# First hidden chunk by plain products, first keys beside the gates, and additions of the down product given priority

## The chip, the cores and the metric

The kernel runs on one core of one Trainium2 chip. The metric is device time in microseconds (us), the median of several executions of the whole program on that core. Three executions of the kernel before gave 1960.85, 1961.96 and 1962.16 us. Engines are named as in the profile: PE (TensorE), PEld (its weight load), DVE (VectorE), ACT (ScalarE), POOL (GpSimd), SP (SyncE, which issues the transfers). A label such as L132 is line 132 of the kernel.

## What is computed

A two-layer encoder over 768 tokens (512 of a prompt, 256 of a sample) of width 1024. Layer 0 mixes tokens by a Fourier transform, layer 1 by a gated delta rule with 8 heads. Behind each mixer stands a SwiGLU block with 2816 hidden units, and each block has a modulated RMS norm ahead of it. All in float32. Cut to what the change touches:

```
def swiglu(h, w_gu, w_down):
    gu = h @ w_gu
    return (silu(gu[..., :2816]) * gu[..., 2816:]) @ w_down

mod = (silu(c) @ ada_w[layer] + ada_b[layer])
sh1, sc1, g1, sh2, sc2, g2 = split(mod, 6)
h = rmsnorm(x, norm_mix_g[layer]) * (1 + sc1) + sh1
x = x + g1 * mixer(h)
h = rmsnorm(x, norm_ffn_g[layer]) * (1 + sc2) + sh2
x = x + g2 * swiglu(h, w_gu[layer], w_down[layer])
```

In the gated delta rule `proj = h @ w_in` gives queries, keys, values, an output gate and 32 columns of gates for the recurrence (4 x 8).

## The kernel before

**Products.** A float32 product is made of three passes in the type fp32r: each operand is split into a high part (a rounded copy, made by ACT) and a low part (the difference, made by DVE or POOL), and PE adds high by high, low by high and high by low in one bank of PSUM (`passes`). Weights come from HBM into a staging tile `stg`, are cast to `wh` by ACT (L151) and to `wl` by DVE (L152), and live in one of five slots (WP = 5) until PE has used them. Matmuls go through the helper at L132. In the changed kernel the same lines are L130, L149 and L150.

**The block of hidden units.** The hidden units are worked through in 22 chunks of 128, in groups that PARTS lists: in layer 0 mostly four chunks at a time, in layer 1 first two, then fours. For each chunk `gate_up` makes gate and up together as a two by two product over halves of the width and halves of the tokens (384 columns each), in a Strassen-Winograd form: 7 half products, each 12 matmuls of 384 columns, 84 in all where the plain form needs 96. Its operand blocks numbered 1 to 7 are made once for a layer by `norm_blocks`: the normalised rows m = 0 to 7 (one of them is 128 features by 768 tokens), the differences of row halves, and the high and low part of each. Blocks 1 and 2 are rows as they are; the others are differences of rows. In each layer the first group is the chunks 0 and 1 side by side, so that PE has two products for every operand that arrives.

**`norm_blocks`.** It takes squares of x, sums them over the features with a product by ones, and then for each m multiplies by the root (L349, on DVE, for m = 7 on POOL), applies scale and shift in two ACT instructions (L352), casts the high part (L199, ACT) and takes the low part (L200, DVE or POOL: the tuples YP, BL and GL name which go to POOL). The order of m is 0, 4, 1, 5, 2, 6, 3, 7, and differences are interleaved.

**The down product.** For each group of four chunks `down4` multiplies by the down weights, in two halves of 512 output columns each; a half is again 7 half products of 12 matmuls, whose results are added into x by `into` (L532, on DVE) as soon as each is complete. A later half product goes on in the same bank of PSUM, so it waits for that addition. Each half runs after the gate and up product of a later chunk, between two of them. Weight casts for down are L497 and L498; differences of weights for gate and up are L379 (one of them on DVE, two on POOL).

**Order.** The order of instructions on each engine is made by a scheduler from the order of the code and priorities: a piece in `tc.high_priority()` goes ahead of others that are ready. Weight casts (L151, L152, L497, L498) and weight differences (L379) have it; the additions at L532 have not. Layer 0 also does the products of the modulation for later blocks (`ada_steps`, tiles `at` of 128 x 512, two matmuls of 256 columns each), which `advance(steps, n)` in `between` deals out among the chunks and the scheduler places.

**Start of the gated delta rule.** The gates product (`pab`, weights at column 4128 - 128) is written first; the queries, keys and values of head h come from `conv_block(h, which, ...)`, one product each.

Of the kernel before, what the change touches and what calls it, by code (L numbers as in the profile page):

```python
# [12 lines left out]
F32 = mybir.dt.float32  # L13
F32R = mybir.dt.float32r
AF = mybir.ActivationFunctionType
# [28 lines left out]
PAIRS = (1, 3, 5)  # L44
YP = (7,)
BL = (0, 1, 2, 3)
GL = (3,)
ST = 4
M7 = 2
WP = 5  # L50
# [59 lines left out]
def encoder_kernel(  # L110
# [87 lines left out]
    def split_to(ah, al, src, eng=None):  # L198
        A_.copy(ah, src)  # L199
        (eng or V).tensor_tensor(al, src, ah.bitcast(F32), ALU.subtract)  # L200
# [133 lines left out]

    def norm_blocks(n, xs, psp, wk, ext, load=True, pairs=False):
# [8 lines left out]
        ts = []  # L344
        for c in range(HK):
            ts.append([])
            for b in range(2):
                t, m = scratch(), c + b * HK
                (G if m in YP else V).tensor_tensor(t, xs[m], rs, ALU.mult)  # L349
                ts[c].append(t)  # L350
                for g, (a, ln) in enumerate(SEGS):
                    A_.activation(t[:, a : a + ln], t[:, a : a + ln], AF.Identity, bias=modT[:, SH[n], m, g : g + 1],  # L352
                                  scale=amod[:, n, m, g : g + 1])
                if b == 0:
                    u, v = 12 + c // 2, slice((c % 2) * HT, (c % 2 + 1) * HT)
                    split_to(eh[u][:, v], el[u][:, v], t[:, lo], G if c in BL else V)
                else:
                    split_to(eh[c], el[c], t, G if c in GL else V)
        for c in range(HK):
            ta, tb = ts[c]  # L360
            t12, t34 = scratch(), scratch()
            V.tensor_tensor(t12[:, lo], ta[:, hi], ta[:, lo], ALU.subtract)
            G.tensor_tensor(t34[:, lo], tb[:, hi], ta[:, hi], ALU.subtract)
            V.tensor_tensor(t12[:, hi], tb[:, hi], t12[:, lo], ALU.subtract)
            G.tensor_tensor(t34[:, hi], tb[:, lo], t12[:, hi], ALU.subtract)
            split_to(eh[4 + c], el[4 + c], t12)
            split_to(eh[8 + c], el[8 + c], t34)
# [5 lines left out]
        return {1: b11, 2: half(0, lo), 3: half(0, hi), 5: half(4, lo), 6: half(4, hi), 7: half(8, lo), 4: half(8, hi)}  # L373

    def gate_up(wgu, ms, blocks, psp, wk):
# [50 lines left out]
        lefts = [left(m) for m in ms]  # L426
        sg = [wk.tile([P, T], F32, name="sg", bufs=3) for _ in ms]
        up = [wk.tile([P, T], F32, name="up", bufs=2) for _ in ms]
# [20 lines left out]
        step(((3, px, False, gate2),))  # L449
        return sg, silu[-1]  # L450

    def residual(x, ps, gate, m):
# [24 lines left out]
    def down4(l, c0, m0, rights, xs, psp, wk):  # L477
# [51 lines left out]
        def into(m, ps, a, b, g):  # L529
            x = xs[m][:, a:b]  # L530
            o = HT if a >= HT else 0
            V.scalar_tensor_tensor(x, ps[:, a - o : b - o], modT[:, gate, m, g : g + 1], x, ALU.mult, ALU.add)  # L532

# [25 lines left out]

    def ffn(l, blocks, xs, psp, wk, gt, between, last, done):  # L560

# [18 lines left out]
        for c0, cn in PARTS[l]:  # L580
# [43 lines left out]
    with ExitStack() as l0:  # L624
# [114 lines left out]
        with ExitStack() as fs:  # L739
# [5 lines left out]
            ppr = fs.enter_context(tc.tile_pool(name="ppr0b", reuse_waits="tile", bufs=6, space=PSUM))  # L745
            blocks = norm_blocks(1, xs, ppr, gt, ext)
            steps = ada((5, 7, 6, 8, 10, 9, 11, 13, 12), psm, apool, 2)
            ffn(0, blocks, xs, ppr, wk, gt, lambda n: advance(steps, n), None,
                lambda m: nc.sync.dma_start(xd[m], xs[m]))
# [9 lines left out]
    with ExitStack() as gs:  # L759
# [141 lines left out]
        def conv_block(h, which, pool, tag, bufs):  # L901
            wb = load_block(win, 0, KC, which * D + h * P)
            pq = product(ppr, wb, hh, hl, KC, tick)
            wc = [cwT[:, d * 24 + which * 8 + h : d * 24 + which * 8 + h + 1] for d in range(5)]
# [288 lines left out]
    with ExitStack() as l1:  # L1193
# [15 lines left out]
        blocks = norm_blocks(3, xs, ppr, gt, ext, False, True)  # L1209

# [77 lines left out]

        ffn(1, blocks, xs, ppr, wk, gt, lambda n: None, finish, None)

# [24 lines left out]
```

## Time and profile before

| what | value |
|---|---|
| median of three executions | 1961.96 us |
| the profiled execution's own time | 1961.55 us |
| span of the profiled execution | 1959.8 us |
| busy ACT, POOL | 977.8 us (50%), 563.7 us (29%) |
| granted PE clock, mean | 0.984 |
| PE products by the high part of a hidden chunk (`pr<-g,wh`, down) | 1072 matmuls, 23.6 us idle before them |

The time stands 1.75 us over the span of the same execution. Busy shares overlap: engines work at the same time, and what sets the time is the engine that the others wait for. In the profile "idle before <- releaser" is how long an engine sat still before an instruction and which instruction let it go on. PEclk is the clock that PE was granted, 1.00 being the full one.

### The profile page before, as it was taken

What the parts mean: (1) busy time and instruction counts of PE and PEld (TensorE: products, weight loads), DVE (VectorE), ACT (ScalarE), POOL (GpSimd) and SP (SyncE); (2) the same over time, 40 slices, a digit from 0 to 9 for tenths busy, and PEclk for the clock granted to TensorE, in tenths of its full rate; (3) what the DMA queues carried; (4) which work ended last, traced back from release to release, by engine and by line L of the source; (5) the groups of instructions that cost most, each with busy time, mean ns of one, the idle gap of its engine ahead of it and who ended that gap; (6) DMA issues with size and microseconds to landing.
All of it is one profiled execution on the core that took longest, in us unless ns stands there. A gap on an engine that the chain in (4) does not pass through costs nothing.

```text
span 1959.8 us, 30027 instructions
## 1 busy us (share of the span) xinstructions
PE 1842.1 (94%) x11281; PEld 1636.7 (84%) x11281; DVE 1468.8 (75%) x2399; ACT 977.8 (50%) x1858; POOL 563.7 (29%) x454
## 2 busy tenths in 40 slices
PE   8899999999999998999999999899789999999998
PEld 5585998888897986888888888778589999999998
DVE  4638877777786767896887787773778888888875
ACT  3526544444443535756656557543554444444543
POOL 1314333233242310122213212320432333433431
PEclk9999999999999998999999999999899999999999
DMA  7654334433425434421222222241213222222211
GB/s 268 215 183 140 86 97 130 127 116 114 139 87 153 126 113 141 119 51 56 69 60 65 66 62 57 61 142 38 53 41 89 68 77 72 65 65 68 77 50 65
DMA packets 231914, 189.72 MB, mean 97 GB/s; under 512 B 20304, under 2 KB 200665, under 8 KB 231769
## 3 DMA queue, kind: packets, MB, share of 16 engines
q1 hardware_dynamic: 231360, 187.66, 31.7%
q8 instruction: 88, 1.44, 0.3%
q14 instruction: 57, 0.47, 0.1%
q10 hardware_dynamic: 409, 0.15, 0.0%
HBM read 174.36 MB, written 13.42 MB: 96 GB/s over the span
## 4 chain that ended last, share of the span: by engine, by line
PE 69%; DVE 14%; ACT 6%; DMA 5%; issue 3%; POOL 3%; ACTq 0%; SPq 0%; DVEq 0%; POOLq 0%
PE pr L132 58%; PE sm L132 8%; DVE wl L152 3%; DVE wa L913 2%; DMA at<-in_ada_w_dram 1%; PE ax L132 1%; DMA cc<-solved 1%; ACT wh L151 1%; POOL yy L1158 1%; DVE we L858 1%; PE big L132 1%; DVE x L532 1%; DVE tmp L1030 1%; ACT we L859 1%; DMA at<-in_final_ada_w_dram 1%
## 5 line engine op out<-in xcount | busy, mean ns | idle before, releaser
L132 PE MATMUL pr<-hh,wh 128*128 128x384 f32 (+2 forms) x1520 | 525.4, 348 | 9.0 <-ACT sg L403 2.3
L132 PE MATMUL pr<-hl,wh 128*128 128x384 f32 (+2 forms) x1520 | 522.8, 344 | 5.2 <-DVE hl L200 4.2
L132 PE MATMUL pr<-hh,wl 128*128 128x384 f32 (+2 forms) x1520 | 520.7, 343 | 1.2 <-DVE wl L152 1.2
L151 ACT CAST wh<-stg 128x512 fp32r<-128x512 f32 (+1 forms) x380 | 230.7, 609 | 394.7 <-PE pr L132 324.3
L152 DVE TENSOR_TENSOR wl<-stg,wh 128x512 fp32r<-128x512 f32 (+1 forms) x380 | 315.2, 832 | 127.7 <-ACT wh L151 124.7
L132 PEld LDWEIGHTS pr<-hh,wh 128*128 128x128 f32 x1520 | 287.7, 190 | 39.8 <-issue 7.4
L132 PEld LDWEIGHTS pr<-hl,wh 128*128 128x128 f32 x1520 | 288.2, 190 | 32.3 <-issue 9.5
L132 PEld LDWEIGHTS pr<-hh,wl 128*128 128x128 f32 x1520 | 287.9, 190 | 24.0 <-issue 6.2
L132 PE MATMUL pr<-g,wh 128*128 128x384 f32 (+2 forms) x1072 | 278.3, 341 | 23.6 <-DVE x L532 13.3
L132 PEld LDWEIGHTS pr<-g,wh 128*128 128x128 f32 x1072 | 191.8, 188 | 37.0 <-DVE x L532 19.8
L379 POOL TENSOR_TENSOR s<-stg 128x512 f32<-128x512 f32 x44 | 62.6, 1423 | 453.4 <-DMA stg<-in_ffn_w_gu_dram 362.7
L132 PE MATMUL pr<-el,wh 128*128 128x384 f32 x528 | 179.9, 341 | 6.4 <-POOL el L200 5.9
L132 PE MATMUL pr<-eh,wh 128*128 128x384 f32 x528 | 181.1, 344 | 3.7 <-ACT eh L199 3.7
L132 PE MATMUL pr<-g,wl 128*128 128x384 f32 (+2 forms) x536 | 181.1, 338 | 0.0
L132 PE MATMUL pr<-eh,wl 128*128 128x384 f32 x528 | 179.2, 339 | 0.0
L498 DVE TENSOR_TENSOR wl<-stg,wh 128x512 fp32r<-128x512 f32 x108 | 99.8, 924 | 36.0 <-ACT wh L497 33.8
L913 DVE SCALAR_TENSOR_TENSOR wa<-pad,cwT,wa 128x770 f32<-128x770 f32 x96 | 109.4, 1140 | 5.2 <-ACT wa L910 3.6
L132 PEld LDWEIGHTS pr<-eh,wh 128*128 128x128 f32 x528 | 100.2, 190 | 12.4 <-issue 7.0
L132 PEld LDWEIGHTS pr<-el,wh 128*128 128x128 f32 x528 | 99.9, 189 | 9.7 <-POOL el L200 8.5
L497 ACT CAST wh<-stg 128x512 fp32r<-128x512 f32 x108 | 67.1, 621 | 81.5 <-PE pr L132 67.1
L132 PEld LDWEIGHTS pr<-g,wl 128*128 128x128 f32 x536 | 101.0, 188 | 0.7
L132 PEld LDWEIGHTS pr<-eh,wl 128*128 128x128 f32 x528 | 99.8, 189 | 0.9 <-issue 0.8
(370 smaller groups left out, 3241.8 us busy)
## 6 DMA issues: line engine op xcount, KB each, us to landing
stg<-in_ffn_w_gu_dram SPq DMA_DIRECT2D x88, 512.0 KB, 4.7
at<-in_ada_w_dram SPq DMA_DIRECT2D x112, 256.0 KB, 3.1
at<-in_ada_w_dram SPq DMA_DIRECT2D x40, 512.0 KB, 4.6
stg<-in_ffn_w_down_dram SPq DMA_DIRECT2D x36, 512.0 KB, 3.7
stg<-in_gdn_w_in_dram SPq DMA_DIRECT2D x33, 512.0 KB, 4.3
at<-in_final_ada_w_dram SPq DMA_DIRECT2D x32, 256.0 KB, 3.6
raw<-gcd SPq DMA_DIRECT2D x8, 768.0 KB, 4.4
stg<-in_fnet_w_dram SPq DMA_DIRECT2D x8, 512.0 KB, 5.1
```

Source lines behind the costliest of these rows:

```text
L132: return nc.tensor.matmul(out, lhsT, rhs, start=start, stop=stop, **kw)
L151: A_.copy(wh[:, :n], src)
L152: V.tensor_tensor(wl[:, :n], src, wh[:, :n].bitcast(F32), ALU.subtract)
L379: eng.tensor_tensor(out, a, b, op)
L497: A_.copy(wh, src)
L498: V.tensor_tensor(wl, src, wh.bitcast(F32), ALU.subtract)
L532: V.scalar_tensor_tensor(x, ps[:, a - o : b - o], modT[:, gate, m, g : g + 1], x, ALU.mult, ALU.add)
L858: V.tensor_scalar(e, src, -44.0, None, ALU.max)
L859: A_.activation(e, e, AF.Exp, scale=-1.0)
L913: V.scalar_tensor_tensor(acc, pad[:, d : d + T + 2], wc[d], acc, ALU.mult, ALU.add)
L1030: se.tensor_tensor(t, r4[:, :, : k + 1, k : k + 1].to_broadcast(sh), u4[:, :, k : k + 1, k + 1 :].to_broadcast(sh), ALU.mult)
L1158: G.tensor_tensor(so, so, sq, ALU.add)
```

## The change

Four edits.

1. The first chunk of each layer is made by a new function, `gate_up_whole`: the plain product, 96 matmuls. Its four results (gate and up, two halves of the tokens) are written k by k, so that the 12 matmuls of a row m can run when that row's high and low parts are there. `norm_blocks` calls it through `early`, between the plain rows and the differences, and takes m in the order 0 to 7. The next group is then chunks 1 and 2 side by side in layer 0, and chunk 1 alone in layer 1.
2. In `norm_blocks` POOL loses the multiplication for m = 7 and five low parts in each layer; they go to DVE. The two differences per row on POOL stay.
3. `into` gets `tc.high_priority()`.
4. The gates product and the first keys' product (both segments of the gates, the first segment of the keys) are written pass by pass beside each other; `conv_block(0, 1)` makes only the second segment.

```diff
-            V.scalar_tensor_tensor(x, ps[:, a - o : b - o], modT[:, gate, m, g : g + 1], x, ALU.mult, ALU.add)
+            with tc.high_priority():
+                V.scalar_tensor_tensor(x, ps[:, a - o : b - o], modT[:, gate, m, g : g + 1], x, ALU.mult, ALU.add)
...
+    def gate_up_whole(wgu, m, plain, psp, wk):
+
+        ws = [load_block(wgu, 0, KC, o + m * P) for o in (0, FFN)]
+        ps = [[bank(psp)[:, :HT] for _ in range(2)] for _ in ws]
+        gens = [passes(p, w, [a[i][0] for a in plain], [a[i][1] for a in plain], skip_group_check=True)
+                for w, pair in zip(ws, ps) for i, p in enumerate(pair)]
+        for _ in zip(*gens):
+            pass
+        sg = wk.tile([P, T], F32, name="sg", bufs=SGB)
+        for i, (a, b) in enumerate(zip(*ps)):
+            v = sg[:, i * HT : (i + 1) * HT]
+            A_.activation(v, a, AF.Silu)
+            V.tensor_tensor(v, v, b, ALU.mult)
+        return sg
...
-            for ms in [(0, 1), *((m,) for m in range(2, cn))] if c0 == 0 else [(c0 + i,) for i in range(cn)]:
+            groups = [(c0 + i,) for i in range(cn)]
+            if c0 == 0:
+                take(0, first)
+                between(AD[0])
+                groups = [(1, 2), *groups[3:]] if cn > 2 else groups[1:]
+            for ms in groups:
...
+        ts, plain = [], []
+        for m in range(KC):
+            t, c = scratch(), m % HK
+            V.tensor_tensor(t, xs[m], rs, ALU.mult)
+            ts.append(t)
+            for g, (a, ln) in enumerate(SEGS):
+                A_.activation(t[:, a : a + ln], t[:, a : a + ln], AF.Identity, bias=modT[:, SH[n], m, g : g + 1],
+                              scale=amod[:, n, m, g : g + 1])
+            if m < HK:
+                u, v = 12 + c // 2, slice((c % 2) * HT, (c % 2 + 1) * HT)
+                split_to(eh[u][:, v], el[u][:, v], t[:, lo])
+                split_to(eh[8 + c][:, hi], el[8 + c][:, hi], t[:, hi])
+                plain.append(((eh[u][:, v], el[u][:, v]), (eh[8 + c][:, hi], el[8 + c][:, hi])))
+            else:
+                split_to(eh[c], el[c], t)
+                plain.append(((eh[c][:, lo], el[c][:, lo]), (eh[c][:, hi], el[c][:, hi])))
+        first = early(plain)
...
-        w = load_block(win, 0, KC, 4128 - P)
-        pab = product(ppr, w, hh, hl, KC)
+
+        w, wk0 = load_block(win, 0, KC, 4128 - P), load_block(win, 0, KC, D)
+        pab, pk0 = ([bank(ppr, 0)] for _ in range(2))
+        pab.append(bank(ppr, 1))
+        for _ in zip(*(passes(p, v, [a[:, lo : lo + ln] for a in hh], [a[:, lo : lo + ln] for a in hl], skip_group_check=True)
+                       for p, v, (lo, ln) in ((pab[0], w, SEGS[0]), (pk0[0], wk0, SEGS[0]), (pab[1], w, SEGS[1])))):
+            pass
```

What the edits move on the engines is seen in their instruction orders.

**VectorE in a half of the down product of layer 0** (the one that ran from 362 to 377 us in the trace of before). The first rows are of before, the second of the change, from the same place. `pr` with a number is one result of a half product in PSUM, `x` the residual it is added to, `wl` and `stg` are weights of the next gate and up chunk.

```order
L152 TENSOR_TENSOR wl_3570<-stg_3565,wh_3569 128x512
L532 SCALAR_TENSOR_TENSOR x_106<-pr_3366,modT_87,x_106 128x128
L379 TENSOR_TENSOR stg_3565<-s1_3604,stg_3565 128x512
L532 SCALAR_TENSOR_TENSOR x_106<-pr_3366,modT_87,x_106 128x256
L532 SCALAR_TENSOR_TENSOR x_106<-pr_3367,modT_87,x_106 128x128
L152 TENSOR_TENSOR wl_3574<-stg_3565,wh_3573 128x512
L532 SCALAR_TENSOR_TENSOR x_106<-pr_3367,modT_87,x_106 128x256
L379 TENSOR_TENSOR stg_3565<-stg_3565 128x512
L532 SCALAR_TENSOR_TENSOR x_106<-pr_3368,modT_87,x_106 128x128
L152 TENSOR_TENSOR wl_3609<-stg_3565,wh_3608 128x512
L532 SCALAR_TENSOR_TENSOR x_106<-pr_3368,modT_87,x_106 128x256
```

```order
L150 TENSOR_TENSOR wl_3574<-stg_3569,wh_3573 128x512
L554 SCALAR_TENSOR_TENSOR x_106<-pr_3370,modT_87,x_106 128x128
L554 SCALAR_TENSOR_TENSOR x_106<-pr_3370,modT_87,x_106 128x256
L385 TENSOR_TENSOR stg_3569<-s1_3608,stg_3569 128x512
L554 SCALAR_TENSOR_TENSOR x_106<-pr_3371,modT_87,x_106 128x128
L554 SCALAR_TENSOR_TENSOR x_106<-pr_3371,modT_87,x_106 128x256
L554 SCALAR_TENSOR_TENSOR x_106<-pr_3372,modT_87,x_106 128x128
L554 SCALAR_TENSOR_TENSOR x_106<-pr_3372,modT_87,x_106 128x256
L150 TENSOR_TENSOR wl_3578<-stg_3569,wh_3577 128x512
L554 SCALAR_TENSOR_TENSOR x_106<-pr_3373,modT_87,x_106 128x128
L554 SCALAR_TENSOR_TENSOR x_106<-pr_3373,modT_87,x_106 128x256
L385 TENSOR_TENSOR stg_3569<-stg_3569 128x512
```

The two additions of one result (128 and 256 columns) stood apart, with a weight operation between them; now they stand together, and the weight cast `wl_3574`, in the change `wl_3578`, comes behind six additions of this half and not behind three.

**ScalarE in the norm of layer 1, from the fourth row to the sixth.** `g` with a number is a row's scratch tile, `eh` and `hh` high parts; `wh_13567` and `wh_13602` are weight casts of chunk 1. In the change:

```order
L350 ACTIVATE g_13351<-g_13351,modT_87,amod_92 128x512
L350 ACTIVATE g_13351<-g_13351,modT_87,amod_92 128x256
L350 ACTIVATE g_13357<-g_13357,modT_87,amod_92 128x512
L197 CAST hh0_71<-g_13351 128x768
L149 CAST wh_13567<-stg_13559 128x512
L350 ACTIVATE g_13357<-g_13357,modT_87,amod_92 128x256
L149 CAST wh_13602<-stg_13559 128x512
L197 CAST hh1_72<-g_13357 128x768
```

Before, no weight cast stands among the rows' instructions there. The five slots are filled by the four weight tiles of chunk 0 and one of chunk 1, so `wh_13567` is the sixth and needs a slot that PE has finished with, and the high part of row 5 (`hh1`) is queued behind it.

**TensorE at the start of the block in layer 0**, before (`sm<-at` are products of the modulation, `eh4`/`el4` the first operand; `ones` is the sum of squares):

```order
L132 MATMUL pr_1431<-g_1422,ones_65 128x256
L132 MATMUL sm_1830<-at_1847,csT_91 32x256 x2
L132 MATMUL sm_1830<-at_1851,csT_91 32x256 x2
L132 MATMUL sm_1830<-at_1855,csT_91 32x256 x2
L132 MATMUL sm_1830<-at_1859,csT_91 32x256 x2
L132 MATMUL sm_1830<-at_1863,csT_91 32x256 x2
L132 MATMUL sm_1830<-at_1867,csT_91 32x256 x2
L132 MATMUL pr_1542<-eh4_1440,wh_1552 128x384
L132 MATMUL pr_1542<-el4_1446,wh_1552 128x384
L132 MATMUL pr_1542<-eh4_1440,wl_1553 128x384
L132 MATMUL sm_1830<-at_1871,csT_91 32x256 x2
```

And in the change, from the same sum of squares on:

```order
L130 MATMUL pr_1431<-g_1422,ones_65 128x256
L130 MATMUL sm_1682<-at_1691,csT_91 32x256
L130 MATMUL sm_1682<-at_1695,csT_91 32x256 x2
L130 MATMUL sm_1682<-at_1699,csT_91 32x256 x2
L130 MATMUL sm_1682<-at_1703,csT_91 32x256 x2
L130 MATMUL sm_1682<-at_1999,csT_91 32x256 x2
L130 MATMUL sm_1682<-at_2003,csT_91 32x256 x2
L130 MATMUL pr_1524<-eh4_1440,wh_1506 128x384
L130 MATMUL sm_1682<-at_2007,csT_91 32x256
L130 MATMUL pr_1525<-eh0_1436,wh_1506 128x384
L130 MATMUL pr_1526<-eh4_1440,wh_1516 128x384
L130 MATMUL pr_1527<-eh0_1436,wh_1516 128x384
```

From the first 384-column matmul of the block up to its 72nd, 33 products of the modulation stand between them before, and 1 in the change; by the 600th there are 68 before and 64 in the change.

More of the change, by code (lines that the diff above doesn't have):

```diff
@@ L44 @@
 PAIRS = (1, 3, 5)
-YP = (7,)
-BL = (0, 1, 2, 3)
-GL = (3,)
 ST = 4
+SGB = 3
 M7 = 2
@@ L343, in norm_blocks @@
         lo, hi = slice(0, HT), slice(HT, T)
-        ts = []
-        for c in range(HK):
[L346 to L358, printed above, removed]
+        ts, plain = [], []
@@ L359, in norm_blocks @@
+        first = early(plain)
+        t12s = []
+        for c in range(HK):
+            ta, tb, t12 = ts[c], ts[HK + c], scratch()
+            V.tensor_tensor(t12[:, lo], ta[:, hi], ta[:, lo], ALU.subtract)
+            V.tensor_tensor(t12[:, hi], tb[:, hi], t12[:, lo], ALU.subtract)
+            split_to(eh[4 + c], el[4 + c], t12)
+            t12s.append(t12)
         for c in range(HK):
-            ta, tb = ts[c]
-            t12, t34 = scratch(), scratch()
-            V.tensor_tensor(t12[:, lo], ta[:, hi], ta[:, lo], ALU.subtract)
+            ta, tb, t34 = ts[c], ts[HK + c], scratch()
@@ L363, in norm_blocks @@
             G.tensor_tensor(t34[:, lo], tb[:, hi], ta[:, hi], ALU.subtract)
[L364 to L367, printed above, removed]
+            G.tensor_tensor(t34[:, hi], tb[:, lo], t12s[c][:, hi], ALU.subtract)
+            split_to(eh[8 + c][:, lo], el[8 + c][:, lo], t34[:, lo])
+            split_to(eh[8 + c][:, hi], el[8 + c][:, hi], t34[:, hi])
@@ L372, in norm_blocks @@
         b11 = tuple([e[12 + c // 2][:, (c % 2) * HT : (c % 2 + 1) * HT] for c in range(HK)] for e in (eh, el))
-        return {1: b11, 2: half(0, lo), 3: half(0, hi), 5: half(4, lo), 6: half(4, hi), 7: half(8, lo), 4: half(8, hi)}
+        return {1: b11, 2: half(0, lo), 3: half(0, hi), 5: half(4, lo), 6: half(4, hi), 7: half(8, lo), 4: half(8, hi)}, first
     def gate_up(wgu, ms, blocks, psp, wk):
@@ L426, in gate_up @@
         lefts = [left(m) for m in ms]
-        sg = [wk.tile([P, T], F32, name="sg", bufs=3) for _ in ms]
+        sg = [wk.tile([P, T], F32, name="sg", bufs=SGB) for _ in ms]
         up = [wk.tile([P, T], F32, name="up", bufs=2) for _ in ms]
@@ L558, in down4, with ffn @@
         run(3, px, False, high(0))
-    def ffn(l, blocks, xs, psp, wk, gt, between, last, done):
+    def ffn(l, blocks, first, xs, psp, wk, gt, between, last, done):
         def whole(c0, cn, gs):
@@ L745, in encoder_kernel @@
             ppr = fs.enter_context(tc.tile_pool(name="ppr0b", reuse_waits="tile", bufs=6, space=PSUM))
-            blocks = norm_blocks(1, xs, ppr, gt, ext)
+            blocks, first = norm_blocks(1, xs, ppr, gt, ext, lambda plain: gate_up_whole(ffn_w_gu[0], 0, plain, ppr, wk))
             steps = ada((5, 7, 6, 8, 10, 9, 11, 13, 12), psm, apool, 2)
-            ffn(0, blocks, xs, ppr, wk, gt, lambda n: advance(steps, n), None,
+            ffn(0, blocks, first, xs, ppr, wk, gt, lambda n: advance(steps, n), None,
                 lambda m: nc.sync.dma_start(xd[m], xs[m]))
@@ L901, in conv_block @@
         def conv_block(h, which, pool, tag, bufs):
-            wb = load_block(win, 0, KC, which * D + h * P)
-            pq = product(ppr, wb, hh, hl, KC, tick)
+            if (h, which) == (0, 1):
+                pq = pk0
+                pq.append(bank(ppr, 1))
+                lo, ln = SEGS[1]
+                for last in passes(pq[1], wk0, [a[:, lo : lo + ln] for a in hh], [a[:, lo : lo + ln] for a in hl]):
+                    tick(T * 3 * 0.421, last)
+            else:
+                wb = load_block(win, 0, KC, which * D + h * P)
+                pq = product(ppr, wb, hh, hl, KC, tick)
             wc = [cwT[:, d * 24 + which * 8 + h : d * 24 + which * 8 + h + 1] for d in range(5)]
@@ L1208, in encoder_kernel @@
             residual(xs[m], po, GATE[2], m)
-        blocks = norm_blocks(3, xs, ppr, gt, ext, False, True)
+        blocks, first = norm_blocks(3, xs, ppr, gt, ext, lambda plain: gate_up_whole(ffn_w_gu[1], 0, plain, ppr, wk), False, True)
         make_amod(4)
@@ L1287, in finish @@
             return True
-        ffn(1, blocks, xs, ppr, wk, gt, lambda n: None, finish, None)
+        ffn(1, blocks, first, xs, ppr, wk, gt, lambda n: None, finish, None)
 _INS = ['x_prompt', 'x_sample', 'c_prompt', 'c_sample', 'ada_w', 'ada_b', 'norm_mix_g', 'norm_ffn_g', 'fnet_w', 'fnet_b',
```

2 lines of the change are left out of this document (1 added, 1 removed).

## The prediction

> **What bounds the kernel now.** I read the page first: busy shares, then the chain of work that ended last.
>
> ```profile
> PE 1842.1 (94%) x11281; PEld 1636.7 (84%) x11281; DVE 1468.8 (75%) x2399; ACT 977.8 (50%) x1858; POOL 563.7 (29%) x454
> PE 69%; DVE 14%; ACT 6%; DMA 5%; issue 3%; POOL 3%; ACTq 0%; SPq 0%; DVEq 0%; POOLq 0%
> ```
>
> PE is busy for 94% of the span, and the chain lies on PE for 69% of it. The change adds matmuls (12 in each layer), so it can only gain where PE stands still or runs at a low clock. The view of PE's waits names its releasers; the first four rows are the additions of the down product (L532) by the tile that they write, the last the weight casts:
>
> ```profile
> PE pr L132 <- DVE x L532: 13.3, 14, 1.9
> PE pr L132 <- DVE vT L532: 6.2, 4, 1.7
> PE pr L132 <- DVE qT L532: 2.0, 4, 0.9
> PE pr L132 <- DVE wa L532: 1.9, 3, 0.7
> ...
> PE pr L132 <- DVE wl L152: 1.2, 2, 0.7
> ```
>
> Together 13.3 + 6.2 + 2.0 + 1.9 = 23.4 us in 25 waits, in 18 halves of the down product (ten in layer 0, eight in layer 1). The next stop is one such half, PE's row and DVE's timeline ahead of it:
>
> ```profile
> 369.95 1.73 DVE L379 TENSOR_TENSOR stg<-stg 128x512 f32<-128x512 f32 x1
> 371.60 0.34 DVE L532 SCALAR_TENSOR_TENSOR x<-pr,modT,x 128x128 f32<-128x128 f32 x1
> 371.87 1.49 DVE L152 TENSOR_TENSOR wl<-stg,wh 128x512 fp32r<-128x512 f32 x1
> 373.28 1.65 DVE L532 SCALAR_TENSOR_TENSOR x<-pr,modT,x 128x256 f32<-128x256 f32 x4
> ...
> 373.81 0.70 PE L132 MATMUL pr<-g,wh 128*128 128x384 f32 x2 [1.90 <-DVE x L532]
> ```
>
> PE stood 1.90 us until an addition of 128x256 that DVE reached only after a weight difference (1.73) and a weight cast (1.49), neither of which PE needed yet. That is the wait the priority in `into` speaks to.
>
> **Term 1, the urgent additions: -24 us.** A wait costs more than its idle time. Three stretches of seven microseconds in layer 1, where no product of the modulation mixes in (PE busy and its matmuls of 384 columns, the clock, DMA; the last has the waits):
>
> ```profile
> 1575.00:1582.00 7.00, 7.00 (x42) 1.00 0.01 3
> 1582.00:1589.00 7.00, 6.99 (x40) 1.00 0.51 150
> 1589.00:1596.00 7.00, 5.52 (x29) 1.00 0.00 0
> ```
>
> Against the middle row 11 matmuls are missing, 11 x 0.175 = 1.9 us, for 7.00 - 5.52 = 1.48 us of idle: a factor of 1.3, as PE's pipeline fills again. So all the waits cost 23.4 x 1.3 = 30.4 us. The half with the wait at 373.81 also lost some clock:
>
> ```profile
> 362.00:377.00 15.00, 13.11 (x69) 12.79 (x68) 13.17 (x22) 4.71 (x9) 6.73 (x6) 0.91 0.23 70
> ```
>
> PEclk is 0.91 there, 15 x 0.09 = 1.4 us; so at most 32 go. What stays: by the new order at most one weight operation stands between a product's end and its addition. That is 0 to 1.73 us by the rows above, where before up to two stood there. I let a quarter to a fifth of 30.4 stay and take -24; the ends are -32 (all) and -12 (half of the waits come back as one stretched operation).
>
> What hides the delayed casts: a cast comes behind six additions instead of three, some 3 x 0.42 = 1.2 us later (the four additions at 373.28 take 1.65), further on five additions, 2.1 us. It still stands three weight sets ahead of PE, 3 x 12 matmuls x 0.1735 = 6.2 us. If that cover is gone, each late cast is a PE wait like the one removed (rivals 1 and 3).
>
> **Term 2, the first chunk of layer 1: -5.5 us.** Windows of before over the norm of layer 1 (columns: PE, PEld, DVE, ACT, POOL busy, then the clock):
>
> ```profile
> 1410.00:1415.00 5.00, 3.76 (x9) 2.44 (x9) 5.00 (x4) 5.00 (x9) 5.00 (x3) 0.50 0.02 3
> 1415.00:1418.70 3.70, 1.07 (x4) 0.74 (x5) 3.70 (x3) 3.70 (x7) 3.70 (x3) 0.96 0.00 0
> 1418.70:1422.10 3.40, 2.80 (x9) 2.29 (x8) 3.40 (x5) 3.40 (x7) 1.97 (x3) 0.50 0.00 0
> 1422.10:1425.50 3.40, 1.72 (x8) 1.39 (x9) 3.30 (x4) 0.27 (x1) 3.40 (x3) 1.00 0.00 0
> 1425.50:1429.00 3.50, 3.02 (x11) 2.23 (x9) 3.40 (x3) 0.00 (x0) 3.50 (x4) 0.51 0.00 0
> 1429.00:1442.00 13.00, 10.79 (x53) 8.88 (x54) 13.00 (x14) 9.08 (x15) 4.86 (x3) 1.00 0.00 0
> 1442.00:1456.00 14.00, 13.96 (x80) 13.65 (x79) 8.57 (x13) 9.80 (x19) 4.72 (x4) 1.00 0.36 96
> ```
>
> Until 1429 PE starves on operands (9 + 4 + 9 + 8 + 11 matmuls in 19 us) and pays half clock in three stretches. The two chunks, 168 matmuls, run from the first to the last of these rows:
>
> ```profile
> 1409.88 0.69 PE L132 MATMUL pr<-eh,wh 128*128 128x384 f32 x1 [3.75 <-ACT eh L199]
> 1455.87 0.34 PE L132 MATMUL pr<-hh,wl 128*128 128x384 f32 x1
> ```
>
> Now the change. ACT sets the pace of the rows:
>
> ```profile
> 1408.12 1.30 ACT L352 ACTIVATE g<-g,modT,amod 128x512 f32<-128x512 f32 x2 [1.03 <-DVE g L349]
> 1409.33 0.50 ACT L199 CAST eh<-g 128x384 fp32r<-128x384 f32 x1
> 1409.73 2.00 ACT L352 ACTIVATE g<-g,modT,amod 128x512 f32<-128x512 f32 x3
> 1421.56 0.81 ACT L199 CAST hh<-g 128x768 fp32r<-128x768 f32 x1
> ```
>
> A row costs it 1.21 (1408.12 to 1409.33) plus two casts of 0.40 (1409.33 to 1409.73) or one of 0.81, some 2.0 us; a row feeds 12 matmuls, 2.08 us at full clock (14.0 / 80 = 0.175 each), 3.8 at half (0.32). So PE can nearly keep step from 1410, but the sixth weight cast is queued ahead of the high part of row 5, waits for PE to end rows 0 to 3, and holds the rows behind it. Worked out by hand: two rows at half clock to 1417, two at full to 1421; then ACT has two weight casts and three rows, some 7.5 us, and DVE ends the last low parts, between weight casts, some 4 to 6 us behind it. So the last operand comes at 1432 to 1435, and the plain product ends near 1435.5. Of chunk 1 some 81 matmuls are then left, 14.1 us, so 180 matmuls end near 1449.5 to 1451 where 168 ended at 1455.9: -5.5. Ends: -9 if the cast doesn't hold, 0 if the differences, which now come after all rows, are late. DVE's added work there (a multiplication, four low parts of 384 columns, one of 768) is bounded by
>
> ```profile
> 1416.45 1.75 DVE L200 TENSOR_TENSOR hl<-g,hh 128x768 fp32r<-128x768 f32 x1
> 1438.42 0.95 DVE L200 TENSOR_TENSOR hl<-g,hh 128x768 fp32r<-128x768 f32 x1
> ```
>
> the first with POOL at work, the second without: 4 operations' worth of 768 columns, 3.8 to 7 us, hidden while ACT sets the pace. The Trainium skill, "SBUF — State Buffer", section "SBUF: two separate sides", has the port pair of the two engines as an exclusive lock; these rows agree, 1.75 against 0.95, and by it POOL's loss of work makes DVE's rows shorter.
>
> The same windows bear on the clock. The longest idle time of PE ahead of the stretch at 1418.7 is
>
> ```profile
> 1418.26 0.45 PE L132 MATMUL pr<-hl,wh 128*128 128x384 f32 x1 [1.87 <-DVE hl L200]
> ```
>
> PE was busy 1.07 of the 3.70 us before, and the next stretch is at 0.50. The Trainium skill, "TensorE: Matmul & The Clock Gate", section "Why this matters for your kernels", asks only for no idle gaps over about 3 us. By that rule the stretch at 1418.7 would have run at full clock and the plain product would too, from 1413 on, some 2 us better, a sum of 1931; the row disagrees, and my sum goes by the row.
>
> **Term 3, the first chunk of layer 0: +1 us.** Here PE has other work in its idle time:
>
> ```profile
> 164.94 0.44 PE L132 MATMUL pr<-eh,wh 128*128 128x384 f32 x1
> ...
> 228.60 0.34 PE L132 MATMUL pr<-hh,wl 128*128 128x384 f32 x1
> ...
> 384.81 0.34 PE L132 MATMUL pr<-hh,wl 128*128 128x384 f32 x1
> 385.07 0.63 PE L132 MATMUL sm<-at,csT 128*32 128x256 f32 x4
> 385.63 0.44 PE L132 MATMUL pr<-hh,wh 128*128 128x384 f32 x1
> ```
>
> The first three chunks (252 matmuls) ran from 164.94 to 228.60. In the change the plain product, held by the same sixth weight slot, ends by hand near 192, and 168 matmuls of 0.1735 follow, 29.2 us: 264 matmuls near 220.5, -8. But the order has 32 products of the modulation fewer in that idle time; they come later, between matmuls of a busy PE. A tile (two of them) costs there 385.63 - 384.81 - 0.17 = 0.65 us: 16 x 0.65 = 10.4, or less where tiles run together; I take 9. -8 + 9 = +1, ends -7 and +6.
>
> **Term 4, the start of the delta rule: 0.** The view of windows has that place:
>
> ```profile
> 761.80:779.00 17.20, 16.37 (x70) 12.55 (x71) 16.64 (x35) 9.07 (x17) 0.00 (x0) 0.90 0.01 2
> ```
>
> PE is idle for 0.83 of 17.2 us. In the order of before the scheduler had already set the three products beside each other, so the edit writes down what was done; bounds -2 and +2.
>
> **Sum.** Against the profiled execution's 1961.55: 1961.55 - 24 - 5.5 + 1 + 0 = **1933**. It lies 0.4 us below the median, which is nothing here.
>
> **Rivals.** (1) *The waits come back as waits for weight casts.* DVE's work in a half does not shrink. In the half from 1581 its busy time is
>
> ```profile
> 1581.00:1595.60 14.60, 13.11 (x71) 11.90 (x71) 14.56 (x25) 5.52 (x9) 6.30 (x5) 1.00 0.25 73
> 1551.50:1566.00 14.50, 13.05 (x75) 12.73 (x74) 12.54 (x23) 5.09 (x9) 5.59 (x4) 1.00 0.21 67
> ```
>
> 14.56 of 14.6 us, and PE needs 84 x 0.1735 = 14.6: no order helps there. The second half has 2 us of slack, which speaks against. If a fifth is all that goes, term 1 is -6: 1961.55 - 6 - 5.5 + 1 = 1951. (2) *The plain product stays at half clock*: rows late by 3.5 us or more, as DVE shares its port, leave PE half busy, as 1.72 of 3.40 at 1422.1 did before a stretch at 0.51. Then a row costs 12 x 0.32 = 3.84: 30.7 us from 1410 on, 1441, and 81 matmuls more end near 1455.9 (term 2: 0); in layer 0 the plain product ends at 195.7 and term 3 is -4 + 10 = +6. 1961.55 - 24 + 6 = 1943.5. Against it: ACT's row of 2.0 us. (3) *Slower: the additions block the casts.* DVE works in order; an addition at its head whose product isn't done holds the casts behind it. Where the lead of 6.2 us is used up, each half has a PE wait of one weight set, 12 x 0.1735 = 2.08 plus 0.28 to fill again: 18 x 2.36 = +42.5 against -30.4, with terms 2 and 3 1961.55 + 12.1 - 4.5 = 1969. It decides from the point at which a cast comes less than one set ahead. Against it: weight casts cost PE next to nothing now (1.2 us in two waits, by the row above). (4) *Both (1) and (2)*: 1961.55 - 6 + 6 = 1961.5, no change.
>
> **How the numbers follow.** The forecast 0.57, rival 1 0.20, rival 2 0.10, rival 3 0.07, rival 4 0.06. The range takes in the bounds of the first term and of the second and reaches to rivals 1 and 2: 1916 to 1953. A measurement of this kernel can tell about 0.2%, 3.9 us, from no change. Faster by more: the forecast and rivals 1 and 2 but for their tails, 0.85. Within: rival 4 and tails, 0.08. Slower by more: rival 3, 0.07.
>
> **What would show it.** Term 1: PE's waits for the additions fall from 23.4 us to 5 or so, and no row for `wl` of more than a few us takes their place; if one does, rival 1 or 3. Term 2: the 180th matmul of 384 columns after the norm of layer 1 comes some 40 us after the first, where the 168th came 46 after; if clock rows of 0.5 cover it all, rival 2. Term 3: the 264th in layer 0 comes 56 us after the first, with lone tiles of the modulation behind it. Term 4: the row of windows stays. I would be wrong above all if DVE, and not its order, sets the halves.

## The result, and the profile after

The changed kernel took 1917.88 us (median of four, 1915.77 to 1920.01) where the kernel before took 1961.95 beside it: a ratio of 0.9776, interval 0.976 to 0.9793. That is 44 us faster; 1933 was forecast with a range of 1916 to 1953.

The page of the profile after, its span, its first line and the chain by engines:

```profile
span 1918.3 us, 30058 instructions
PE 1831.7 (95%) x11305; PEld 1640.5 (86%) x11305; DVE 1435.5 (75%) x2415; ACT 976.1 (51%) x1860; POOL 541.9 (28%) x436
PE 71%; DVE 15%; ACT 6%; DMA 3%; issue 3%; POOL 2%; ACTq 0%; DVEq 0%; SPq 0%; POOLq 0%
```

PE has 24 matmuls more and is busy 10 us less; the mean clock granted to it is 0.989 after 0.984, and 0.005 of the span is about as much. No run separates the clock's part from the rest. DVE's busy time fell too, by 33 us, though it took work over from GpSimd. Some 9 of them go by the experiment on GpSimd's share; the priority alone brings 12, and the change has six weight casts and four differences fewer on DVE.

In the view of PE's waits no row names the additions any more (L554 now; 23.4 us before). These rows stand for the weight casts and for one wait that has no row in the view of before, that of PE for ACT's copy of a half product in the gate and up product (L409):

```profile
PE pr L130 <- ACT up L409: 1.3, 3, 0.4
...
PE pr L130 <- DVE wl L150: 1.0, 2, 0.7
```

The weight casts took nothing over (1.2 us before, 1.0 now). The view of the additions in the trace of after lists who waited for them, us in total and times:

```profile
  ACT wh L149: 8.3, 6
  POOL s L513: 7.9, 6
  POOL s L385: 2.5, 2
```

PE isn't among them. The windows over the norm of layer 1 (PE, PEld, DVE, ACT, POOL busy; then the clock) answer to those of before from 1410 to 1456:

```profile
1385.00:1387.00 2.00, 1.67 (x5) 1.45 (x6) 2.00 (x5) 2.00 (x5) 0.00 (x0) 0.50 0.00 0
1387.00:1390.40 3.40, 3.40 (x13) 3.40 (x12) 3.40 (x7) 3.40 (x8) 0.00 (x0) 0.50 0.00 0
1390.40:1393.80 3.40, 3.40 (x18) 3.40 (x18) 3.40 (x7) 3.40 (x8) 0.75 (x1) 0.83 0.00 0
1393.80:1397.20 3.40, 3.40 (x22) 3.40 (x21) 2.59 (x5) 2.16 (x4) 3.40 (x2) 1.00 0.00 0
1397.20:1402.00 4.80, 3.74 (x22) 3.42 (x22) 4.65 (x6) 4.80 (x9) 2.83 (x3) 1.00 0.00 0
1402.00:1409.50 7.50, 4.80 (x26) 4.17 (x26) 7.50 (x7) 3.14 (x6) 5.22 (x4) 1.00 0.00 0
```

One start at half clock (5.4 us, then 0.83 for a window), then full speed; before there were three stretches at half clock. The first matmul of the block and the 180th after the norm of layer 1, the ends of the 39.8 us in the table below:

```profile
1385.33 1.10 PE L130 MATMUL pr<-eh,wh 128*128 128x384 f32 x2 [4.27 <-ACT eh L197]
...
1425.08 0.33 PE L130 MATMUL pr<-hh,wh 128*128 128x384 f32 x1
```

The span by stages, from the starts of the same matmuls in each trace (us; the third column is a second profile of the changed kernel, from the experiments):

| stage | before | change | change again |
|---|---|---|---|
| start to the first matmul of the block in layer 0 | 164.9 | 167.8 | 163.9 |
| block of layer 0, to the next sum of squares | 590.0 | 573.7 | 573.3 |
| delta rule, to the 1920th matmul of its products | 628.0 | 623.9 | 623.1 |
| from there to the last sum of squares of layer 1 | 22.9 | 15.4 | 15.4 |
| to the first matmul of the block | 4.1 | 4.6 | 4.6 |
| chunks 0 and 1 (168 matmuls, in the change 180) | 46.0 | 39.8 | 39.7 |
| the rest of the block, to the final norm | 463.1 | 452.4 | 451.1 |
| final norm | 40.8 | 40.8 | 40.8 |

The start differs from before by 2.8 us one way and 1.0 the other between two profiles of one kernel, so it isn't the change. The row from the delta rule to the last sum of squares, 7.5 us shorter, belongs to no term of the prediction. The delta rule's row also differs between kernels that are alike there; its experiment has the spread.

### The profile page after: what moved, and what is told of

Read it like the earlier page. It is cut to its first block, busy times and chain, and to the rows that moved or that the text cites. A ratio compares the mean times of both kernels' runs of the same rounds, so it can differ in the third digit from the quotient of the medians.

```text
span 1918.3 us, 30058 instructions
## 1 busy us (share of the span) xinstructions
PE 1831.7 (95%) x11305; PEld 1640.5 (86%) x11305; DVE 1435.5 (75%) x2415; ACT 976.1 (51%) x1860; POOL 541.9 (28%) x436
## 4 chain that ended last, share of the span: by engine, by line
PE 71%; DVE 15%; ACT 6%; DMA 3%; issue 3%; POOL 2%; ACTq 0%; DVEq 0%; SPq 0%; POOLq 0%
PE pr L130 58%; PE sm L130 9%; DVE wa L952 2%; DVE wl L150 2%; PE ax L130 1%; PE big L130 1%; DMA at<-in_ada_w_dram 1%; ACT wh L149 1%; DVE hl L198 1%; DMA cc<-solved 1%; DVE stg L385 1%; POOL yy L1197 1%; DVE we L890 1%; ACT we L891 1%; DVE x L554 1%
## 5 line engine op out<-in xcount | busy, mean ns | idle before, releaser
L130 PE MATMUL pr<-hh,wl 128*128 128x384 f32 (+2 forms) x1520 | 519.4, 342 | 1.0 <-DVE wl L150 1.0
L150 DVE TENSOR_TENSOR wl<-stg,wh 128x512 fp32r<-128x512 f32 (+1 forms) x376 | 297.9, 795 | 119.4 <-ACT wh L149 116.0
L130 PE MATMUL pr<-g,wh 128*128 128x384 f32 (+2 forms) x1072 | 273.6, 337 | 0.0
```

The costliest lines, as they stand in the source:

```text
L130: return nc.tensor.matmul(out, lhsT, rhs, start=start, stop=stop, **kw)
L150: V.tensor_tensor(wl[:, :n], src, wh[:, :n].bitcast(F32), ALU.subtract)
```

## Experiments

The theory after the result: the additions' waits went altogether (some 29 us); the plain chunk of layer 1 gains twice, behind the norm and ahead of it; layer 0's first chunk is a draw; the delta rule's edit is worth a few us. The rivals to each part stand in the expectations. "Over the changed kernel" is measured by ratios, since each run has its own runs of the kernel before beside it.

**The priority alone.**

```diff
-            V.scalar_tensor_tensor(x, ps[:, a - o : b - o], ...)
+            with tc.high_priority():
+                V.scalar_tensor_tensor(x, ps[:, a - o : b - o], ...)
```

> The kernel before with the priority in `into` and nothing else. Theory A (the 25 waits for the additions are all that the priority touches, and each costs 1.3 times its idle time): the waits for L532 go to under 1 us, the two stretches behind the first chunks shorten by 12 and 11 us or a little more, the delta rule and the norm of layer 1 keep their times; 1962 - 23 to - 30 = 1932 to 1939 us. Theory B (the priority also brings the 4 us of the delta rule and the 7 us ahead of the norm of layer 1): about 1925 us. Theory C (the waits come back as waits for weight casts unless the first chunk is plain too): 1950 us or more.

Measured 1930.05 us against 1958.74: 28.7 us, ratio 0.9855 (0.9841 to 0.9869). No row of PE's waits names the additions. Layer 0 from its first matmul to the next norm went from 590.0 to 572.0, the rest of layer 1 from 463.1 to 453.0, 18.0 + 10.1 = 28.1; the stretch ahead of the norm of layer 1 was 24.6 (22.9), the delta rule 625.1 (628.0). Theory A, with layer 0 gaining more than its 12 us and the whole 2 us more than its range.

**The change without the priority.**

```diff
-            with tc.high_priority():
-                V.scalar_tensor_tensor(x, ps[:, a - o : b - o], ...)
+            V.scalar_tensor_tensor(x, ps[:, a - o : b - o], ...)
```

> The changed kernel with the additions back at plain priority. Theory A: the additions' waits are there again, some 23 us of idle time on PE, and the rest keeps its gain: 1918 + 23 to + 30 = 1941 to 1948 us. Theory B: 1955 us, with the delta rule at its old length.

1944.15 us, ratio 0.9929 (0.9914 to 0.9944), 0.0153 or 30 us over the change. The waits are back (the line is L553 in this kernel):

```profile
PE pr L130 <- DVE x L553: 12.3, 15, 1.6
...
PE pr L130 <- DVE vT L553: 4.4, 4, 1.2
```

with 2.4, 1.8 and 0.2 us on the other three tiles 21.1 us in all, and the delta rule keeps its length (621.6). Theory A. By both runs a microsecond of such waiting costs 28.7 / 23.4 = 1.2 to 30 / 21.1 = 1.4 us.

**The start of the delta rule, undone and alone.**

```diff
-        w, wk0 = load_block(win, 0, KC, 4128 - P), load_block(win, 0, KC, D)
...
+        w = load_block(win, 0, KC, 4128 - P)
+        pab = product(ppr, w, hh, hl, KC)
```

> The changed kernel with the gates product and the first keys written one after the other as before. Theory A (the 4 us that the delta rule is shorter come from this edit): 1922 us, and the stretch from the first product of the delta rule to the last products of its output is 4 us longer than in the changed kernel, most of it within the first 60 us. Theory B (the scheduler laid the three products beside each other anyway, and the 4 us are waits that fell another way as the order shifted): 1918 us, within 2.

1919.27 us, ratio 0.9794 (0.978 to 0.9809): 0.0018 or 3.5 us over the change, but the intervals overlap. Its delta rule took 626.0, against 623.9 and 623.1. That lies between the two theories and settles nothing by itself. So the edit went alone into the kernel before:

> The kernel before with the gates product and the first keys written beside each other, and nothing else. Theory A (this edit brings the 3 us by which the delta rule is shorter in the profiles that have it): from the first sum of squares ahead of the delta rule to the 1920th matmul of its products 621 to 624 us and not 623 to 628, the whole 2 to 4 us under the kernel before. Theory B (the difference is in other waits that move from kernel to kernel): within 1.5 us of the kernel before, 624 us or more for that stretch.

1954.67 us against 1961.58, ratio 0.9974 (0.9962 to 0.9986), 2.7 to 7.5 us; the delta rule took 622.5. Theory A. In nine profiles with the edit that stretch takes 621.5 to 623.9, mean 622.4; in five without it 623.4 to 628.0, mean 625.5. The gain doesn't lie at the products that the edit touches, nor within the first 60 us where theory A of the run above had it. Up to 69 us after the sum of squares both kinds keep step; then comes this wait of PE, in the row of before, and in the change the same transposes without it:

```profile
826.42 0.63 PE L943 MATMUL ax<-ident,vT 128*128 128x128 f32 x4 [1.13 <-DVE vT L917]
```

```profile
811.71 0.63 PE L982 MATMUL ax<-ident,vT 128*128 128x128 f32 x4
```

The wait (1.11 to 1.13 us) stands in each of the five profiles without the edit and in none of the nine with it. It is a third of the 3.1 us between the means; where the other 2 us lie was not found. Why is not settled either: the first head's keys now tell the planner of the delta rule all their PE time in the second segment, which moves what it lays between, but that was not tried by itself.

**The norm of layer 1: what precedes it.** Before, DVE's row of instructions there reads (timeline, start and duration):

```profile
1383.91 0.69 DVE L379 TENSOR_TENSOR stg<-s,stg 128x512 f32<-128x512 f32 x1 [3.21 <-POOL stg L379]
1384.52 0.74 DVE L454 SCALAR_TENSOR_TENSOR qT<-pr,modT,qT 128x512 f32<-128x512 f32 x1
1385.18 1.36 DVE L152 TENSOR_TENSOR wl<-stg,wh 128x512 fp32r<-128x512 f32 x1
1387.72 0.69 DVE L379 TENSOR_TENSOR stg<-s,stg 128x512 f32<-128x512 f32 x1 [1.19 <-POOL stg L379]
1388.33 0.48 DVE L454 SCALAR_TENSOR_TENSOR qT<-pr,modT,qT 128x256 f32<-128x256 f32 x1
```

DVE stands 3.21 us for GpSimd's part of a weight difference, with the residual additions (L454) that the norm needs behind it in its queue. (Of the four differences of a gate and up chunk two are on DVE and two on GpSimd, by the code and by 88 each in the trace of before; the section on the kernel before has one on DVE.) In the change the first chunk has no differences, and the same additions read:

```profile
1363.47 0.75 DVE L475 SCALAR_TENSOR_TENSOR qT<-pr,modT,qT 128x512 f32<-128x512 f32 x1 [0.40 <-PE pr L130]
...
1366.30 0.48 DVE L475 SCALAR_TENSOR_TENSOR qT<-pr,modT,qT 128x256 f32<-128x256 f32 x1 [0.19 <-PE pr L130]
```

They wait for their product alone. A first try gave those additions priority in the kernel before:

```diff
-            residual(xs[m], po, GATE[2], m)
+            with tc.high_priority():
+                residual(xs[m], po, GATE[2], m)
```

> The kernel before with priority for the eight residual additions of the delta rule's output product, ahead of the norm of layer 1; nothing else. Theory A (the norm of layer 1 starts 7 us sooner in the changed kernel because VectorE no longer has differences of weights, waiting for GpSimd, ahead of those additions): the last sum of squares comes 5 to 7 us sooner, 1955 to 1957 us. Theory B (PE, ACT or the transfers set that stretch): 1962 us, within 2.

1962.79 us against 1958.74, ratio 1.0023 (1.0014 to 1.0032), and the stretch grew from 22.9 to 27.9. Its time lies in theory B's range, but it neither bears out A nor refutes it: the scheduler left both differences where they were, the first behind a wait of 3.21 us again, and pulled the additions of later rows ahead of those of earlier ones (the second part of `pad` came at 1391.53, behind those of `we` and `wa`), so that the first sum of squares came 18.1 us after the 1920th matmul and not 13.3. Then the differences were held by an explicit order:

```diff
-            with tc.high_priority():
+            with tc.issue_after(held_back[0].ins) if held_back and eng is V else tc.high_priority():
                 eng.tensor_tensor(out, a, b, op)
...
-            residual(xs[m], po, GATE[2], m)
+            last = residual(xs[m], po, GATE[2], m)
+        held_back.append(last)
```

> The kernel before, with VectorE's weight differences of the first two chunks of layer 1 held until after the last residual addition of the delta rule's output; weight casts stay where they are. Theory A (differences that wait for GpSimd stand ahead of the residual additions on VectorE, and these are what the norm waits for): the last sum of squares comes 4 to 7 us sooner, the 168 matmuls take as long as before or up to 2 us longer, 3 to 7 us under the kernel before. Theory B (the casts, ACT or the transfers set the stretch): within 2 us of the kernel before.

1954.33 us against 1960.78, ratio 0.997 (0.9959 to 0.998), 4 to 8 us. The stretch went to 16.8, 6.1 us shorter, and the 168 matmuls still took 46.0. Its DVE:

```profile
1375.67 0.75 DVE L456 SCALAR_TENSOR_TENSOR qT<-pr,modT,qT 128x512 f32<-128x512 f32 x1 [0.20 <-PE pr L132]
...
1389.22 1.90 DVE L379 TENSOR_TENSOR stg<-s,stg 128x512 f32<-128x512 f32 x2
```

Theory A: the additions come with their product, the differences 13 us behind the first of them, and the 168 matmuls take no longer for it.

**The first chunks of layer 1 as before**, in the change (the old norm, and chunks 0 and 1 side by side):

```diff
-        blocks, first = norm_blocks(3, xs, ppr, gt, ext, lambda plain: gate_up_whole(...), False, True)
+        blocks, first = norm_blocks_old(3, xs, ppr, gt, ext, False, True), None
...
+            if c0 == 0 and first is None:
+                groups = [(0, 1), *groups[2:]]
```

> The changed kernel with the norm and the first two chunks of layer 1 as before. Theory A (the plain chunk is worth 6 us after the norm and 7 us ahead of it, since the casts and differences of two chunks are no longer made ahead of the residual additions): the stretch up to the last sum of squares goes from 15.4 back to 22 to 24 us, 168 matmuls take 46 us again, in all 12 to 14 us over the changed kernel. Theory B (only the rows' arrival counts): 5 to 7 us over the changed kernel.

1932.52 us, 15.8 over the change beside it (1916.75). The stretch ahead of the norm is 23.0 again (15.4 in the change), 168 matmuls take 46.0 (39.7 for 180), and the rest of the block 454.2 (451.1), 3 us that theory A didn't have. Theory A, and more than its 12 to 14 us. The old norm brings GpSimd's share back as well, so this run prices the plain chunk and the share together.

The change itself, beside it:

> The changed kernel once more, beside the three others, for a second profile. It should come at 0.976 to 0.979 of the kernel before. The start (up to the first sum of squares) and the delta rule (first product to the 1920th) should differ from the first profile by what the transfers do to them: theory B of the third experiment wants the delta rule to move by 2 us or more between profiles of one kernel, theory A wants it within 1 us of 616.9.

1916.75 us, ratio 0.9772 (0.9755 to 0.9789); the delta rule, counted from its first product, took 616.0 (616.9), the start 3.9 us less than in the first profile. The delta rule moved by 0.9 us between the two profiles, as its expectation has it under theory A.

**GpSimd's share of the norm given back.**

```diff
-            V.tensor_tensor(t, xs[m], rs, ALU.mult)
+            (G if m in YP else V).tensor_tensor(t, xs[m], rs, ALU.mult)
...
-                split_to(eh[u][:, v], el[u][:, v], t[:, lo])
+                split_to(eh[u][:, v], el[u][:, v], t[:, lo], G if c in BL else V)
...
-                split_to(eh[c], el[c], t)
+                split_to(eh[c], el[c], t, G if c in GL else V)
```

> The changed kernel with GpSimd taking the multiplication for m = 7 and the five low parts of each norm back. Theory A (GpSimd at work slows VectorE, and its own operations take 1.3 to 2.5 us, so the rows come later): 180 matmuls in layer 1 take 41 to 44 us and not 39.7, the first 264 in layer 0 0 to 3 us longer, in all 2 to 8 us over the changed kernel. Theory B (VectorE's work is what the rows wait for): 2 to 4 us under the changed kernel.

1930.41 us, ratio 0.985 (0.9828 to 0.9873): 0.0078 or 15 us over the change: the way of theory A, but twice what it allowed. Layer 1's 180 matmuls took 45.5, layer 0's first 264 took 59.6 (53.9), its whole block 582.0 (573.3). The two engines side by side in the norm of layer 1, in this kernel:

```profile
1390.48 1.35 DVE L201 TENSOR_TENSOR el<-g,eh 128x384 fp32r<-128x384 f32 x1
...
1394.31 2.18 DVE L201 TENSOR_TENSOR el<-g,eh 128x384 fp32r<-128x384 f32 x1
```

```profile
1389.78 1.65 POOL L201 TENSOR_TENSOR el<-g,eh 128x384 fp32r<-128x384 f32 x1 [5.43 <-ACT eh L200]
1391.80 1.77 POOL L201 TENSOR_TENSOR el<-g,eh 128x384 fp32r<-128x384 f32 x1 [0.38 <-ACT eh L200]
1393.53 2.56 POOL L350 TENSOR_TENSOR g<-qT,g 128x768 f32<-128x768 f32 x1
```

DVE takes 1.35 to 2.18 us for a low part of 384 columns, where the change, with GpSimd idle, does two in 1.02:

```profile
1386.06 1.02 DVE L198 TENSOR_TENSOR el<-g,eh 128x384 fp32r<-128x384 f32 x2
```

Over the whole kernel VectorE is busy longer here with 12 operations fewer, 1444.7 us against 1435.5:

```profile
PE 1831.6 (95%) x11305; PEld 1642.7 (85%) x11305; DVE 1444.7 (75%) x2403; ACT 976.8 (51%) x1860; POOL 558.2 (29%) x448
```

The windows of the same stretch, to the end of the plain product, show the clock too:

```profile
1390.00:1400.00 10.00, 7.08 (x28) 6.03 (x28) 10.00 (x8) 8.82 (x17) 9.62 (x6) 0.78 0.00 0
1400.00:1410.00 10.00, 8.68 (x39) 8.35 (x39) 8.38 (x12) 5.09 (x9) 5.79 (x5) 0.83 0.00 0
1410.00:1420.00 10.00, 6.55 (x27) 6.23 (x28) 9.71 (x7) 5.06 (x8) 7.53 (x5) 0.83 0.00 0
```

Without this edit the plain chunk would have gained 48.1 - 45.5 = 2.6 us behind the norm of layer 1 instead of 8.4 (both counted at 180 matmuls). The reverse, GpSimd kept out of the old norm with chunks 0 and 1 side by side, was not tried, so how much of the gain needs the plain chunk at all stays open.

**The sixth weight cast.** In the change ACT shows it (timeline of layer 1's norm), and a kernel took the two early casts' priority away:

```profile
1395.65 0.62 ACT L149 CAST wh<-stg 128x512 fp32r<-128x512 f32 x1 [1.24 <-PE pr L130]
```

```diff
-        with tc.high_priority():
+        with ExitStack() if late else tc.high_priority():
             A_.copy(wh[:, :n], src)
...
-            yield parts(a11)
-            yield parts(a12)
+            yield parts(a11, late)
+            yield parts(a12, late)
```

> The changed kernel with the first two weight casts of the chunk behind the plain one at plain priority, so that ScalarE and VectorE come to them after the rows. Theory A (the sixth weight cast, waiting for a slot, holds the rows behind it): 180 matmuls in layer 1 take 36 to 38.5 us, 2 to 6 us under the changed kernel. Theory B (the plain product's end is then followed by a wait for these casts): the 96 matmuls of the plain product come sooner, the 180 as late or later, 0 to 5 us over the changed kernel.

1924.27 us, ratio 0.9815 (0.9792 to 0.9839), 0.0043 or 8 us over the change. The last of the 96 matmuls of the plain product was issued 1404.37 - 1380.35 = 24.0 us after the first in the second profile of the change, 1406.53 - 1384.85 = 21.7 here; then PE stood:

```profile
1414.00 0.69 PE L130 MATMUL pr<-hh,wh 128*128 128x384 f32 x1 [3.88 <-ACT wh L149]
```

180 took 44.3. In layer 0, where the chunks 1 and 2 had the same casts late, the first 264 took 61.0 (53.9). Theory B, beyond its 5 us: the cast holds the rows for 2 us, and too late a cast costs more.

**Layer 0.** The products of the modulation put back into the idle time of its norm:

```diff
+            def early(plain):
+                advance(steps, 12)
+                return gate_up_whole(ffn_w_gu[0], 0, plain, ppr, wk)
```

> The changed kernel with twelve steps of the modulation written ahead of the plain product of layer 0, so that about 36 of its matmuls are placed in the idle time there as before. Theory A (deferring them cost about 10 us on a busy PE): the stretch behind the 264th matmul of layer 0 shortens by 8 to 12 us, the first 264 take 0 to 4 us more, in all 4 to 10 us under the changed kernel. Theory B (the idle time is too small or the transfers of the modulation's weights hold back the chunk weights): the first 264 lose what the rest gains, within 2 us of the changed kernel.

1914.71 us, ratio 0.9765 (0.9748 to 0.9783), no difference from the change beside it that the intervals allow (0.9772). The first 264 matmuls took 58.8 (53.9), the rest of the block 514.3 (519.4): +4.9 and -5.1. Theory B. The likely reason, not tried by itself, is that with rows arriving every 2 us there is little idle time left to fill. Then layer 0 was set back to the old norm and first chunks, and in layer 1 the difference of chunk 1 was held as above:

```diff
-            blocks, first = norm_blocks(1, xs, ppr, gt, ext, lambda plain: gate_up_whole(...))
+            blocks, first = norm_blocks_old(1, xs, ppr, gt, ext), None
...
-            with tc.high_priority():
+            with tc.issue_after(held_back[0].ins) if held_back and eng is V else tc.high_priority():
```

> The changed kernel with the norm and first chunks of layer 0 as before, and in layer 1 the weight difference of chunk 1 on VectorE held until after the last residual addition. The stages tell the two apart. Theory A (in layer 0 the plain chunk and the later products of the modulation cancel, 1 us against the change; in layer 1 the difference ahead of the last additions costs 1.5 to 2 us): layer 0 from its first matmul to the next norm takes 571 to 573 us and not 573.4, the stretch to the last sum of squares 13.4 to 14 us and not 15.4, in all 1 to 4 us under the changed kernel. Theory B (the plain chunk in layer 0 is a gain of its own): layer 0 takes 577 us or more.

1912.44 us, ratio 0.976 (0.9737 to 0.9783). Layer 0 took 571.6 from its first matmul (573.3), as A had it: the edits to its norm and first chunks, taken together, are a loss of 1.7 us there. It is close to a draw, since four profiles with the layer 0 of the change lie between 572.6 and 573.9. Holding the difference gave nothing (15.4 as before it), against A: in the change the last residual additions weren't waiting for it. None of the runs beats the change by more than the intervals allow; this one and the one before have the lowest ratios.

## Why the prediction came out as it did

The direction, the order of the terms and the range were right; the likeliest value was 15 us too high. By its own terms:

- **Urgent additions, -24 forecast: right in mechanism, sized too small.** Alone they gave -28.7, within the term's ends. The step that failed is "I let a quarter to a fifth of 30.4 stay": nothing stayed. The factor of 1.3 was good (1.2 to 1.4, in which what the waits cost in clock is contained). That one weight operation may still stand ahead of an addition is true, and costs nothing: by the code 18 matmuls lie between a result and the next use of its bank, six for the other bank of its half product and the 12 of another half product, 18 x 0.1735 = 3.1 us. The two additions of a result take 0.73 of these. What is left covers one weight operation, 0.69 to 2.32 us in the trace of before, but not the 1.73 and 1.49 that stood together ahead of the wait at 373.81. This reading was argued from the code and the rows, not tried by itself. The casts' lead held, as forecast; rivals 1 and 3 are out.
- **First chunk of layer 1, -5.5 forecast: right.** 180 matmuls in 39.7 where 168 took 46.0, -6.2. The working by hand held too: a sixth cast that stops ACT (1.24 us), the plain product ending 24.0 us after its first matmul where 25.5 was worked out. Rival 2 is out, but only since GpSimd was kept out of the norm: with it the clock was 0.78 to 0.83 to the product's end, and 180 took 45.5. The prediction bounded that edit at 3.8 to 7 us of hidden work on DVE and didn't see that 0.5 of the 6.2 us would be left if GpSimd kept its share. So the number came out of two edits together, where the prediction credited it to the plain product alone, with ACT setting the pace. What the release of GpSimd would bring without the plain product is open.
- **What was left out: the weights of the first chunk are made ahead of the norm too.** The prediction counted the change's weight work only behind the norm. Before, two chunks' differences stood ahead of the last residual additions on DVE and held the norm back by 6 to 7.5 us; the experiment that only held the differences got 6.1 of it, with no other edit.
- **First chunk of layer 0, +1 forecast: right, partly by luck.** +1.7 by the run that undid it. The two sides were larger than thought, -10 in the first chunks (53.9 for 264 matmuls against 64.0 for 252) and +12 behind them (519.4 against 507.6), and the errors of 2 and 3 us took each other out. Here too the term rests on GpSimd's release: with its share given back the block of layer 0 took 582.0.
- **Start of the delta rule, 0 forecast: wrong by 3 to 5 us.** "The edit writes down what was done" was true of the products that it names, and the first 69 us show no difference; the gain came where the order of the first head's work moved. The bounds of 2 us either way were too narrow: an edit that changes what a planner is told is not bounded by the rows at its own place.

The measured parts, -28.7, -15.8 (layer 1, both sides), +1.7 and -5.1, add up to -47.9 against -44.1; each has an interval of some 2 to 3 us, so the rest is not explained further. The measured time lies only 2 us inside the lower end of the range. Three misses went the same way: 4.7 us of the first term, some 7 us ahead of the norm of layer 1, and 3 to 5 us of the delta rule.

## To carry to other kernels

When an engine that works in order has urgent and patient work in one queue, count how many patient operations can stand ahead of an urgent one, and compare their sum with the cover that the consumer has: here one operation under the cover cost nothing that the waits show, and where more stood ahead the time lost was 1.2 to 1.4 times the wait. When work is removed at one place, look for where it was prepared: a scheduler may have put the preparation ahead of something else, tens of microseconds earlier. And an operation moved from GpSimd to VectorE can make VectorE finish sooner (9 us less busy with 12 operations more), so such a move is to be priced by the neighbours' durations with and without GpSimd, not by the operation alone.

## What the runs showed of the hardware

The rows of the experiment on GpSimd's share (two low parts in 1.02 us alone; 1.35 to 2.18 each while GpSimd works) show the price of company, and how it comes about. GpSimd's operations from 1389.78 and from 1393.53 end at 1391.43 and 1396.09; VectorE's low parts that began beside them end at 1391.83 and 1396.49, 0.40 us later both times, however long they had stood. So VectorE's operation is held until GpSimd's has ended, and not slowed in proportion. The trace of before has the same for weight casts of 128x512: 0.69 us without GpSimd at work, and of 144 that began while a GpSimd operation was under way 141 ended 0.55 us behind its end. The additions of the down product, which read one operand from PSUM, aren't held: 0.47 us for 128x256 columns with GpSimd at work (19 of them) and without. The Trainium skill, "SBUF — State Buffer", section "SBUF: two separate sides", says that the two engines take turns at a shared pair of ports and that the loser waits for a whole instruction of the other; these ends fit that, and that it is the ports the traces don't show.

The clock stayed at 1.00 with PE busy 4.80 of 7.50 us (1402 to 1409.5, its longest idle time there 1.39 us), where before 1.72 of 3.40 was followed by a stretch at 0.51. The border is not sharp in these traces: 1.86 of 3.40 (55%, from 1391.4 in the change without the priority) and 1.63 of 3.40 (48%, from 1376.3 with the start of the delta rule as before) were followed by stretches at 1.00. PE's busy time of such a stretch was not varied by itself in any run.
